# Down projection's operands on the weight plan, steps between units, last units by banks, attention's factor at the output

## The chip, the cores and the metric

The kernel runs on one core of a Trainium2 chip. A core has a matrix engine (PE in the profile; PEld is its weight load), a vector engine (DVE), a scalar engine (ACT), GpSimd (POOL) and a sync engine (SP). Here SP starts nearly all loads and stores, POOL starts those that add into their destination, and all of them are moved by the same 16 DMA engines. Matrix products are accumulated in PSUM, from where only DVE and ACT read them here. The metric is device time in microseconds; smaller is better.

## The reference, cut to what matters

One encoder layer on 512 tokens of width 2048, in float32:

```python
xn = rms_norm(x, attn_norm_g)
u_val, u_gate, q, k, v = split(xn @ w_in)              # 2048 x 5120
y_conv = silu(layer_norm(depthwise31(u_val * sigmoid(u_gate))))      # 1024 wide: group A
y_na = attention(q, k, v, rpb)   # 16 heads of 64, window 8 x 16 on an 8 x 64 grid: group B
x = x + concat(rms_norm(y_conv, conv_out_g), rms_norm(y_na, na_out_g)) @ w_out
gate, val = split(depthwise3(rms_norm(x, ffn_norm_g) @ w_up))         # 2048 x 11264
x = x + (silu(gate) * val) @ w_down                    # 5632 x 2048
return rms_norm(x, final_norm_g)
```

`rms_norm` divides every token's row by one number, so the factor of a token may as well be applied behind the matrix product that follows.

## The kernel before

Activations lie transposed (channels on partitions, 512 tokens along the free axis) up to the down projection, whose results lie with tokens on partitions. For accuracy every operand of a large product is split into a rounded high part and a rest, and a product is three matmuls (`mm3`, lines 126 to 128; `feed`, 728 to 730).

**Weights.** The weights come in units of 128 x 1024. `plan` is a list of functions, one for each unit in the order of use; `weights()` (147) hands out the next unit and first makes those up to `AHEAD = 3` further: a load by SP into one of seven `raw` buffers, the high part by ACT (L115) and the rest by DVE (L116), four buffers of each. A maker of the high part waits, where the buffer it writes is still read, for PE.

**Order.** The order of instructions on each engine comes from a scheduler that follows program order, priorities and its own estimates, so instructions that are written one behind the other may stand in another order, but each engine then works its list off strictly. Side work is written as generators in `steps` and `asteps`; `tick` (133) runs one step of each behind the last matmul of a unit.

**Stages.** (1) The input projection, 80 units in `project`; between them the convolution (`gated`, L311), group A's norms (`group_a`) and attention by head pairs (`attend`): `scores` takes both halves of a pair's scores into the two-bank PSUM tile `sc`, loads two bias tables `tab` by SP (L403), adds them (L407) and exponentiates; `turn` transposes, `values` multiplies by V. `attend` leaves its result in `aos`. (2) The output projection, `out_half(ma, read_a)` and then `out_half(mb, after)`, 16 units each. Between them `norm_b` computes the factor of group B's norm, multiplies the eight tiles of `aos` by it (L501) and splits them (L182, L183) into `mb`, the operands of the second half. `after` adds a product to `x2` (L540), squares it, transposes it to DRAM (`xt`) and makes the operands of (3). (3) The up projection, 44 blocks `f`, each as seven products of half size (a Strassen scheme) of 24 matmuls; then the convolution of width 3, silu and the product with the gate. The first 36 results go to DRAM by SP (L667), the last eight stay; `again` brings the 36 back during the last block by SP (L678). (4) The down projection, again seven products, each of 22 units; `product2` takes a unit and its `operand` (L708 on ACT, L709 on DVE, with one to three sums ahead of them), multiplies it into four PSUM banks, and takes the last `TAIL = 3` units bank by bank. Between products the results are added to the residual (`onto`, L754), and for finished ones `ready` squares (L773) and scales by the norm's weights (L774), `write` computes the token factors (L778 to L785), scales (L791 on DVE, L793 on ACT) and stores by SP (L795). All of this is written between the calls of `product2`.

The sums of two quarters of `w_down` that the scheme needs are made in DRAM by POOL: `sum_ahead` (170) issues a copy and an accumulating load (L176, L177), 88 jobs in all, one behind each of two in three units of the input projection, each second unit of the output projection and each block of the up projection until none is left.

Of the kernel before, what the change touches and what calls it, by code (L numbers as in the profile page):

```python
# [10 lines left out]
F32 = mybir.dt.float32  # L11
F32R = mybir.dt.float32r
AF = mybir.ActivationFunctionType
# [3 lines left out]
P = 128  # L17
# [35 lines left out]
Q = D // 2 // S  # L53
TAIL = 3
ROW = 2048
# [15 lines left out]
def layer(ctx: ExitStack, tc: tile.TileContext, xT, w_in, w_out, w_up, w_down, par, tab, g3, out):  # L71
# [17 lines left out]
    def t2(name, dt=F32):  # L89
        return tp.tile([P, S], dt, tag="t2k", name=name)  # L90
# [181 lines left out]
    def project(n):  # L272
        ps = psm.tile([P, S], F32, tag="mm", name="pj")
        for u in range(KD // U):
            w = weights()
            for k in range(U):
                kk = u * U + k
                m = mm3(ps, w, k, xs[kk][0], xs[kk][1], kk == 0, kk == KD - 1)
            tick(m)
            if weights.at > 6 and weights.at % 3:  # L280
                sum_ahead(m)
            while late:
                late.pop()()
        return ps
# [63 lines left out]

    aos = []
    acc_na = t2("accna")  # L350
# [26 lines left out]
    def attend(p, q, k, v):  # L377
# [14 lines left out]
        def scores(b0):  # L392
# [8 lines left out]
            for j in range(2):  # L401
                tb = t2("tab").rearrange("p (i k) -> p i k", i=2)
                i = nc.sync.dma_start(tb, tab[2 * p + j][:, b0 // 2:b0 // 2 + 2])  # L403
                if p == 0:
                    pin(i)
                s = t2("s").rearrange("p (i k) -> p i k", i=2)
# [27 lines left out]
        def values(b0):  # L434
            for i in range(2):
                b = b0 + i
                for ch in range(2):
                    for j in (1, 0):
# [3 lines left out]
                        if (i, ch, j) != (0, 0, 1):  # L442
                            pin(m)

        yield
        scores(0)
        yield
        yield
        scores(2)
# [46 lines left out]
    mb, wait = [], []  # L496
# [103 lines left out]
    for c in TURN2:  # L600
        for k in order2:
            plan.append(lambda c=c, k=k: unit(wsum[c][k] if c in wsum else w_down[k, {0: A22, 3: A11, 5: A12}[c]],
                                              U * P))

# [65 lines left out]

    back = [f for p in range(2) for f in range(p, NF - KEEP, 2)]

    def again(at, i):
        for _ in range(8):
            if back:
                f = back.pop(0)
                hs[f] = t2("h")
                behind(nc.sync.dma_start(hs[f], hd[f]), i)  # L678

    def paced(at, i):  # L680
        if at == 3:
            sum_ahead(i)

    for f in range(NF):
        hidden(f, again if f == NF - 1 else paced)
    assert not jobs and not back

    def operand(c, k):  # L690
# [19 lines left out]
        return t  # L710

    def four(first):

        if first:
            b = psa.tile([P, 2, S], F32, tag="sc", name="pd2")
            return [psa.tile([P, S], F32, tag="tr", name="pd", bufs=2) for _ in range(2)] + [b[:, 0], b[:, 1]]
        return [psm.tile([P, S], F32, tag="mm", name="pd") for _ in range(3)] + [psa.tile([P, S], F32, tag="po",
                                                                                         name="pd")]

    def product2(c, ps, more):  # L720
        got = []

        def feed(w, h, i, start, stop):
# [5 lines left out]
            nc.tensor.matmul(ps[i], h[:, t], wl[:, d], start=False, stop=False, skip_group_check=more)  # L729
            nc.tensor.matmul(ps[i], h[:, tl], wh[:, d], start=False, stop=stop, skip_group_check=more)  # L730
# [20 lines left out]

    def onto(x, ps):
        for a, b in zip(x, ps):
            add(a, a, b)  # L754
        return x

    gs = []
    for d in range(2 * Q):
        g = t2("g3")
        nc.sync.dma_start(g, g3[:, d * S:(d + 1) * S])  # L760
        if d >= Q:
            nc.vector.tensor_scalar(g, g, -1.0, None, op0=ALU.mult)
        gs.append(g)

    sq = [sm.tile([P, 2, 2 * Q], F32, tag="sq", name="sq") for _ in range(2)]

    def ready(y, th, dh):

        for i in range(2 * Q):
# [6 lines left out]
    def write(th, ys):  # L776
        v, r, y = (sm.tile([P, 2], F32, tag="rs" + c, name="rs" + c) for c in "vry")
        nc.vector.tensor_reduce(v, sq[th], axis=AX.X, op=ALU.add)  # L778
        nc.vector.tensor_scalar(v, v, 1.0 / D, EPS, op0=ALU.mult, op1=ALU.add)
# [5 lines left out]
        nc.vector.tensor_mul(y, y, r)  # L785
        for i in range(2 * Q):
            t, d = divmod(i, Q)
            for dh in range(2):
                x, f = ys[dh][i], y[:, t:t + 1]
                if dh:  # L790
                    nc.vector.tensor_scalar(x, x, f, None, op0=ALU.mult)  # L791
                else:
                    nc.scalar.activation(x, x, AF.Copy, scale=f)  # L793
                o = (Q * dh + d) * S
                nc.sync.dma_start(out[(2 * th + t) * P:(2 * th + t + 1) * P, o:o + S], x)  # L795

    a = four(True)
    product2(3, a, False)
    e3 = onto(rest(0, 0), a)
    b = four(False)  # L800
    product2(0, b, False)
    e0 = onto(rest(0, 1), b)
    product2(4, a, True)
    e4 = onto(rest(1, 0), a)
    b = four(False)
    product2(1, b, False)
    e1 = onto(rest(1, 1), b)
# [72 lines left out]
```

## Time and profile before

| | |
|---|---|
| median of 3 runs | 2069.67 us (2060.13 to 2070.61) |
| profiled execution | 2068.41 us |
| its span, first to last instruction | 2066.6 us |
| PE busy | 2011.7 us (97%) |
| DVE busy | 1588.8 us (77%) |
| ACT busy | 1019.7 us (49%) |
| moved by DMA | 445 MB, mean 215 GB/s |

"Busy" of PE is no measure of speed: a matmul's record overlaps the next, and its length doubles where the granted clock is halved. So the stages are read by windows: so many matmuls in so many microseconds, at such a clock. A wait row names the waiting instruction, then what ended the wait, the total, the count and the longest.

### The profile page before, as it was taken

How to read it: one execution, taken by the hardware profiler on the slowest of the kernel's cores; microseconds unless marked ns; L12 is line 12 of the kernel's file. 1: busy time of each engine (PE TensorE's matmuls, PEld its weight loads, DVE VectorE, ACT ScalarE, POOL GpSimd, SP SyncE). 2: the span in 40 equal slices, each digit the busy share in tenths (PEclk: the TensorE clock that was granted, in tenths of full speed). 3: DMA queues.
4: the chain of work that ended last, by engine and by line, in shares of the span. 5: the costliest groups of instructions: out<-in, count | busy, mean ns of one | idle time of the engine just before them, and what ended most of it. 6: DMA issues, size and time to landing. Idle time of an engine off the chain costs nothing.

```text
span 2066.6 us, 32277 instructions
## 1 busy us (share of the span) xinstructions
PE 2011.7 (97%) x12620; PEld 1799.9 (87%) x12620; DVE 1588.8 (77%) x2201; ACT 1019.7 (49%) x1548; POOL 202.8 (10%) x270
## 2 busy tenths in 40 slices
PE   8999999999999999999999999999999899999897
PEld 6878888877777899999999999999999688888776
DVE  7985797586566778888888888888888798874764
ACT  6234424446435655555545555554545544554553
POOL 0111111111111111111111100000010000000000
PEclk9999999999999999999999999999999999999999
DMA  6688788778868989998999977677677965666462
GB/s 230 183 242 215 195 214 210 216 198 250 246 165 217 237 229 244 255 242 247 250 253 243 247 189 201 190 193 202 182 188 205 334 208 200 207 211 203 160 214 95
DMA packets 143689, 444.97 MB, mean 215 GB/s; under 512 B 15792, under 2 KB 23984, under 8 KB 142128
## 3 DMA queue, kind: packets, MB, share of 16 engines
q1 hardware_dynamic: 104112, 304.48, 43.0%
q0 software_dynamic: 39424, 138.43, 32.6%
q8 instruction: 99, 1.62, 0.3%
q14 instruction: 54, 0.44, 0.1%
HBM read 425.02 MB, written 110.10 MB: 259 GB/s over the span
## 4 chain that ended last, share of the span: by engine, by line
PE 91%; DVE 4%; DMA 2%; ACT 1%; issue 1%; SPq 0%; ACTq 0%; DVEq 0%
PE pu L126 14%; PE pu L127 14%; PE pu L128 14%; PE pd L728 7%; PE pd L729 7%; PE pd L730 7%; PE pj L126 6%; PE pj L128 5%; PE pj L127 5%; PE po L126 3%; PE po L127 3%; PE po L128 3%; DMA tab<-in_tab 2%; DVE y L311 1%; DVE wlo L116 1%
## 5 line engine op out<-in xcount | busy, mean ns | idle before, releaser
L115 ACT ACTIVATE whi<-raw 128x1024 fp32r<-128x1024 f32 x574 | 605.1, 1057 | 824.9 <-PE pj L127 216.3
L116 DVE TENSOR_TENSOR wlo<-raw,whi 128x1024 fp32r<-128x1024 f32 x574 | 700.6, 1223 | 283.0 <-ACT whi L115 247.6
L126 PE MATMUL pu<-xc,whi 128*128 128x256 f32 x2464 | 697.3, 283 | 1.3 <-ACT uu L633 1.3
L127 PE MATMUL pu<-xc,whi 128*128 128x256 f32 x2464 | 697.7, 283 | 0.0
L128 PE MATMUL pu<-xc,wlo 128*128 128x256 f32 x2464 | 697.2, 283 | 0.0
L126 PEld LDWEIGHTS pu<-xc,whi 128*128 128x128 f32 x2464 | 473.0, 192 | 1.7 <-ACT uu L633 1.7
L127 PEld LDWEIGHTS pu<-xc,whi 128*128 128x128 f32 x2464 | 473.0, 192 | 0.4 <-issue 0.2
L128 PEld LDWEIGHTS pu<-xc,wlo 128*128 128x128 f32 x2464 | 473.0, 192 | 0.2 <-issue 0.2
L728 PE MATMUL pd<-whi,ho 128*128 128x512 f32 x616 | 242.6, 394 | 19.6 <-ACT ho L708 19.6
L126 PE MATMUL pj<-xh,whi 128*128 128x512 f32 x640 | 253.5, 397 | 8.2 <-ACT whi L115 8.2
L128 PE MATMUL pj<-xh,wlo 128*128 128x512 f32 x640 | 250.0, 391 | 1.1 <-DVE wlo L116 1.0
L127 PE MATMUL pj<-xl,whi 128*128 128x512 f32 x640 | 250.7, 392 | 0.0
L729 PE MATMUL pd<-wlo,ho 128*128 128x512 f32 x616 | 242.0, 393 | 0.0
L730 PE MATMUL pd<-whi,ho 128*128 128x512 f32 x616 | 241.2, 393 | 0.0
L311 DVE SCALAR_TENSOR_TENSOR y<-ch,prm,y 128x507 f32<-128x507 f32 (+14 forms) x240 | 169.8, 739 | 3.1
L728 PEld LDWEIGHTS pd<-whi,ho 128*128 128x128 f32 x616 | 117.2, 190 | 44.9 <-ACT ho L708 20.7
L126 PEld LDWEIGHTS pj<-xh,whi 128*128 128x128 f32 x640 | 120.5, 188 | 36.5 <-ACT whi L115 9.5
L128 PEld LDWEIGHTS pj<-xh,wlo 128*128 128x128 f32 x640 | 120.5, 188 | 28.3 <-DVE wlo L116 2.5
L127 PEld LDWEIGHTS pj<-xl,whi 128*128 128x128 f32 x640 | 120.6, 188 | 24.4 <-issue 0.7
L730 PEld LDWEIGHTS pd<-whi,ho 128*128 128x128 f32 x616 | 116.7, 190 | 25.3 <-DVE ho L709 1.1
L729 PEld LDWEIGHTS pd<-wlo,ho 128*128 128x128 f32 x616 | 117.1, 190 | 24.3
L177 POOL DMA_DIRECT2D ws<-in_w_down x88 | 79.1, 899 | 483.2 <-DMA ws<-in_w_down 270.8
(158 smaller groups left out, 2017.6 us busy)
## 6 DMA issues: line engine op xcount, KB each, us to landing
raw<-in_w_up SPq DMA_DIRECT2D x220, 512.0 KB, 5.1
ws<-in_w_down POOLq DMA_DIRECT2D x132, 512.0 KB, 7.0
raw<-in_w_up POOLq DMA_DIRECT2D x88, 512.0 KB, 7.6
raw<-ws SPq DMA_DIRECT2D x88, 512.0 KB, 4.3
raw<-in_w_in SPq DMA_DIRECT2D x80, 512.0 KB, 5.4
raw<-in_w_down SPq DMA_DIRECT2D x66, 512.0 KB, 4.3
ws<-ws POOLq DMA_DIRECT2D x44, 512.0 KB, 6.0
raw<-in_w_out SPq DMA_DIRECT2D x32, 512.0 KB, 5.2
```

The lines of the kernel that those rows point to most:

```text
L115: i = nc.scalar.activation(hi[:, :n], raw[:, :n], AF.Copy)
L116: j = nc.vector.tensor_sub(lo[:, :n], raw[:, :n], hi[:, :n].bitcast(F32))
L126: nc.tensor.matmul(ps, hi[:, a], mh, start=start, stop=False, skip_group_check=more)
L127: nc.tensor.matmul(ps, hi[:, a], ml, start=False, stop=False, skip_group_check=more)
L128: return nc.tensor.matmul(ps, lo[:, a], mh, start=False, stop=stop, skip_group_check=more)
L177: nc.gpsimd.dma_start(wsum[c][k], w_down[k, b], accum_op=ALU.add, max_dma_last_dim=ROW)
L311: nc.vector.scalar_tensor_tensor(y[:, a:b], h[:, a + j - PAD:b + j - PAD], prm[:, o + j:o + j + 1], y[:, a:b], op0=ALU.mult, op1=ALU.add)
L728: nc.tensor.matmul(ps[i], h[:, t], wh[:, d], start=start and not more, stop=False, skip_group_check=more)
L729: nc.tensor.matmul(ps[i], h[:, t], wl[:, d], start=False, stop=False, skip_group_check=more)
L730: nc.tensor.matmul(ps[i], h[:, tl], wh[:, d], start=False, stop=stop, skip_group_check=more)
```

## The change

- `operand(c, k)` moves into `plan`: it is made with its weight unit, three units before use, from within the last block of the up projection on.
- What follows a product of the down projection (`taken`, `ready`, `write`, and the loading of the norm's weights, `factors3`) is written as generators and run a step behind each unit of the next product.
- Only the last product is ended bank by bank, over `TAIL = 4` units; a bank's result is finished and, after each second bank, 128 tokens are normalised and stored while the other banks are multiplied. `write` handles 128 tokens, not 256. `four(True)` lists the two-bank tile first. Half of the stores go by POOL (`queues`), and the 36 loads of `again` too.
- `norm_b` only computes the factor; each `attend` splits its result at once, and `after` multiplies each product by the factor (new L547) before adding.
- The bias tables are loaded one step before the scores that they are added to (`table`).
- `sum_ahead` is called behind each second unit of the input projection and each third of the output projection, so more of its jobs fall into the up projection.

```diff
-            if weights.at > 6 and weights.at % 3:
+            if weights.at > 6 and weights.at % 2:
                 sum_ahead(m)
...
-                tb = t2("tab").rearrange("p (i k) -> p i k", i=2)
-                i = nc.sync.dma_start(tb, tab[2 * p + j][:, b0 // 2:b0 // 2 + 2])
+                tb = tabs.pop(0)
...
+        table(0)
         yield
         scores(0)
         yield
+        table(2)
         yield
         scores(2)
...
-        aos.append(ao)
+        mb.append(split(ao, pc("nag", p), "mb"))
...
-            if d % 2:
+            if d % 3 == 0:
                 sum_ahead(i)
...
-        r = yield from rsqrt_steps(acc_na, NA, "rna")
-        for i in range(NP_):
-            nc.vector.tensor_mul(aos[i], aos[i], r)
-            mb.append(split(aos[i], pc("nag", i), "mb"))
+        rb.append((yield from rsqrt_steps(acc_na, NA, "rna")))
...
-        nc.vector.tensor_add(x2[d], x2[d], ps)
+        t = t2("oa")
+        nc.vector.tensor_mul(t, ps, rb[0])
+        nc.vector.tensor_add(x2[d], x2[d], t)
...
-            plan.append(lambda c=c, k=k: unit(wsum[c][k] if c in wsum else ..., U * P))
+            plan.append(lambda c=c, k=k: (unit(wsum[c][k] if c in wsum else ..., U * P), operand(c, k)))
...
-                behind(nc.sync.dma_start(hs[f], hd[f]), i)
+                behind(nc.gpsimd.dma_start(hs[f], hd[f]), i)
...
-            return [psa.tile(...) for _ in range(2)] + [b[:, 0], b[:, 1]]
+            return [b[:, 0], b[:, 1]] + [psa.tile(...) for _ in range(2)]
...
-        n = NK - TAIL
-        for j, k in enumerate(order2[:n]):
-            w, h = weights(), operand(c, k)
+        n = NK - TAIL if c == TURN2[-1] else NK
+        for j in range(n):
+            w, h = weights()
             for i in range(2 * Q):
-                feed(w, h, i, j == 0, False)
-        got = [(weights(), operand(c, k)) for k in order2[n:]]
-        for i in range(2 * Q):
-            for j, (w, h) in enumerate(got):
-                feed(w, h, i, False, j == TAIL - 1)
+                m = feed(w, h, i, j == 0, j == NK - 1)
+            tick(m)
+        if n < NK:
+            got = [weights() for _ in range(NK - n)]
+            for i in range(2 * Q):
+                for j, (w, h) in enumerate(got):
+                    feed(w, h, i, False, j == NK - n - 1)
+                yield i
...
+    def ready(x, ps, th, dh, only=range(2 * Q)):
+        for i in only:
             t, d = divmod(i, Q)
             d += Q * dh
+            add(x[i], x[i], ps[i])
             q = t2("sq")
-            nc.scalar.activation(q, y[i], AF.Square, accum_out=sq[th][:, t, d:d + 1])
-            nc.vector.tensor_mul(y[i], y[i], gs[d])
+            nc.scalar.activation(q, x[i], AF.Square, accum_out=sq[th][:, t, d:d + 1])
+            nc.vector.tensor_mul(x[i], x[i], gs[d])
+            yield
+
+    queues = [nc.sync, nc.gpsimd]
...
-                nc.sync.dma_start(out[(2 * th + t) * P:(2 * th + t + 1) * P, o:o + S], x)
+                queues[dh].dma_start(out[(2 * th + t) * P:(2 * th + t + 1) * P, o:o + S], x)
+                yield
...
-    product2(2, a, True)
-    for y, th in ((e0, 0), (e1, 1)):
-        ready(onto(y, a), th, 1)
-    product2(6, b, True)
-    ready(onto(e4, b), 1, 0)
+    run(2, a, True)
+    steps += [ready(e0, a, 0, 1), ready(e1, a, 1, 1)]
+    run(6, b, True)
+    steps += [ready(e4, b, 1, 0), write(1, 0, (e4, e1)), write(1, 1, (e4, e1))]
     a = four(True)
-    write(1, (e4, e1))
-    product2(5, a, False)
-    ready(onto(e3, a), 0, 0)
-    write(0, (e3, e0))
+    for i in product2(5, a, False):
+        for _ in ready(e3, a, 0, 0, (i,)):
+            pass
+        if i % Q == Q - 1:
+            for _ in write(0, i // Q, (e3, e0)):
+                pass
```

More of the change, by code (lines that the diff above doesn't have):

```diff
@@ L53 @@
 Q = D // 2 // S
-TAIL = 3
+TAIL = 4
 ROW = 2048
@@ L443, in values, with table @@
                             pin(m)
+        tabs = []
+        def table(b0):
+            for j in range(2):
+                tb = t2("tab").rearrange("p (i k) -> p i k", i=2)
+                i = nc.sync.dma_start(tb, tab[2 * p + j][:, b0 // 2:b0 // 2 + 2])
+                if p == 0:
+                    pin(i)
+                tabs.append(tb)
+        table(0)
         yield
@@ L601, in layer @@
         for k in order2:
[L602 to L603 removed]
+            plan.append(lambda c=c, k=k: (unit(wsum[c][k] if c in wsum else w_down[k, {0: A22, 3: A11, 5: A12}[c]],
+                                               U * P), operand(c, k)))
     out_half(mb, after)
@@ L669, in hidden @@
             hs[f] = g
[L671 to L677, printed above, removed]
-                behind(nc.sync.dma_start(hs[f], hd[f]), i)
[L680 to L686, printed above, removed]
     def operand(c, k):
@@ L710, in operand, with again, paced @@
         return t
+    back = [f for p in range(2) for f in range(p, NF - KEEP, 2)]
+    def again(at, i):
+        for _ in range(8):
+            if back:
+                f = back.pop(0)
+                hs[f] = t2("h")
+                behind(nc.gpsimd.dma_start(hs[f], hd[f]), i)
+    def paced(at, i):
+        if at == 3:
+            sum_ahead(i)
+    for f in range(NF):
+        hidden(f, again if f == NF - 1 else paced)
+    assert not jobs and not back
     def four(first):
@@ L715, in four @@
             b = psa.tile([P, 2, S], F32, tag="sc", name="pd2")
-            return [psa.tile([P, S], F32, tag="tr", name="pd", bufs=2) for _ in range(2)] + [b[:, 0], b[:, 1]]
+            return [b[:, 0], b[:, 1]] + [psa.tile([P, S], F32, tag="tr", name="pd", bufs=2) for _ in range(2)]
         return [psm.tile([P, S], F32, tag="mm", name="pd") for _ in range(3)] + [psa.tile([P, S], F32, tag="po",
@@ L785, in write, with run, then @@
         nc.vector.tensor_mul(y, y, r)
[L786 to L787 removed]
+        for d in range(Q):
             for dh in range(2):
[L789 removed]
+                x = ys[dh][t * Q + d]
                 if dh:
[L791 removed]
+                    nc.vector.tensor_scalar(x, x, y, None, op0=ALU.mult)
                 else:
[L793 removed]
+                    nc.scalar.activation(x, x, AF.Copy, scale=y)
                 o = (Q * dh + d) * S
[L795 removed]
+                queues[dh].dma_start(out[(2 * th + t) * P:(2 * th + t + 1) * P, o:o + S], x)
+                yield
+    def run(c, ps, more):
+        for _ in product2(c, ps, more):
+            pass
+    def then(*g):
+        for x in g:
+            yield from x
     a = four(True)
[L798 to L799 removed]
+    steps.append(factors3())
+    run(3, a, False)
+    e3 = rest(0, 0)
+    steps.append(taken(e3, a))
     b = four(False)
[L801 to L804, printed above, removed]
[L805 to L817 removed]
+    run(0, b, False)
+    e0 = rest(0, 1)
+    steps.append(taken(e0, b))
+    run(4, a, True)
+    e4 = rest(1, 0)
+    steps.append(taken(e4, a))
+    b = four(False)
+    run(1, b, False)
+    e1 = rest(1, 1)
+    steps.append(taken(e1, b))
+    run(2, a, True)
+    steps += [ready(e0, a, 0, 1), ready(e1, a, 1, 1)]
+    run(6, b, True)
+    steps += [ready(e4, b, 1, 0), write(1, 0, (e4, e1)), write(1, 1, (e4, e1))]
+    a = four(True)
+    for i in product2(5, a, False):
[3 more added lines that the diff above has]
+            for _ in write(0, i // Q, (e3, e0)):
+                pass
 def _cols(a):
```

39 lines of the change are left out of this document (18 added, 21 removed).

## The prediction

> **What bounds the kernel now.** I read the page's first part, then windows by stage, then PE's waits, then the timeline at each wait.
>
> ```profile
> span 2066.6 us, 32277 instructions
> PE 2011.7 (97%) x12620; PEld 1799.9 (87%) x12620; DVE 1588.8 (77%) x2201; ACT 1019.7 (49%) x1548; POOL 202.8 (10%) x270
> ```
>
> Windows: length, then each engine's busy time and count, granted PE clock, DMA share and rate.
>
> ```profile
> core 0: us, PE busy (x) PEld busy (x) DVE busy (x) ACT busy (x) POOL busy (x), PEclk, DMA share, GB/s
> 732.00:1170.00 438.00, 438.00 (x3647) 437.54 (x3646) 361.12 (x412) 228.07 (x306) 69.60 (x87) 1.00 0.93 247
> 1170.00:1608.00 438.00, 438.00 (x3653) 438.00 (x3651) 361.27 (x409) 226.44 (x303) 34.78 (x40) 1.00 0.73 199
> 1617.00:1622.70 5.70, 5.68 (x13) 4.44 (x14) 1.73 (x5) 5.02 (x17) 0.00 (x0) 0.50 1.04 399
> 1630.00:1918.00 288.00, 288.00 (x1272) 238.50 (x1271) 227.86 (x377) 139.00 (x196) 0.00 (x0) 1.00 0.62 210
> ```
>
> The up projection runs at 438/3647 = 0.120 us for each 256-wide matmul from end to end, the down projection at 288/1272 = 0.2264 us for a 512-wide one; behind a long wait the clock is 0.50 and a matmul takes 5.70/13 = 0.44 us. PE is the bound, and only what is not at this pace can be won:
>
> ```profile
> 142.90:144.10 1.20, 0.51 (x4) 0.10 (x4) 1.20 (x3) 1.20 (x4) 0.00 (x0) 1.00 1.27 437
> 451.40:454.40 3.00, 0.98 (x5) 0.35 (x4) 1.38 (x3) 1.71 (x6) 0.00 (x0) 1.00 0.83 307
> 503.40:514.00 10.60, 6.49 (x26) 4.59 (x24) 4.92 (x9) 4.84 (x13) 0.88 (x1) 0.68 0.98 316
> 531.90:534.50 2.60, 1.15 (x9) 0.48 (x9) 1.23 (x1) 2.32 (x4) 0.47 (x1) 1.00 0.76 291
> 598.80:606.00 7.20, 3.67 (x10) 2.60 (x10) 6.93 (x11) 1.67 (x2) 0.41 (x1) 0.76 0.84 216
> 1607.90:1623.00 15.10, 6.32 (x17) 4.84 (x17) 8.50 (x15) 8.86 (x22) 0.00 (x0) 0.66 1.04 390
> 1918.90:1931.00 12.10, 5.14 (x15) 3.48 (x14) 11.82 (x21) 10.97 (x32) 0.00 (x0) 0.72 0.37 119
> 1987.90:1996.00 8.10, 4.20 (x14) 2.91 (x13) 7.79 (x16) 7.55 (x18) 0.00 (x0) 0.79 0.62 174
> 2053.70:2066.60 12.90, 0.02 (x1) 0.00 (x0) 5.32 (x15) 4.10 (x9) 0.00 (x0) 0.61 0.43 163
> ```
>
> Where the clock stayed at 1.00 the loss is the idle time: 0.7, 2.0 and 1.4 us. Elsewhere it is the length less the work at full pace (the first two of a count began before the window): at 598.8, 7.2 - 8 x 0.2264 = 5.4; at 1607.9, 15.1 - 14 x 0.2264 - 0.12 = 11.8; at 1918.9, 12.1 - 13 x 0.2264 = 9.2; at 1987.9, 8.1 - 12 x 0.2264 = 5.4; at 503.4, with eight 512-wide and sixteen small matmuls at 0.12, 10.6 - 3.7 = 6.9. The last 12.9 us have no matmul. PE's waits name the causes:
>
> ```profile
> PE pd L728 <- ACT ho L708: 19.6, 3, 8.8
> PE sc L397 <- DVE s L407: 4.1, 1, 4.1
> PE po L126 <- DVE oa L509: 3.5, 1, 3.5
> PE st L326 <- DVE su L413: 2.0, 1, 2.0
> ```
>
> **The change part by part. First unit of the down projection (11.8 us).** ACT, then DVE:
>
> ```profile
> 1608.16 1.06 ACT L115 ACTIVATE whi<-raw 128x1024 fp32r<-128x1024 f32 x1 [1.77 <-PE pu L127]
> 1616.57 1.32 ACT L708 ACTIVATE ho<-uy 128x256 fp32r<-128x256 f32 x4
> 1609.25 1.22 DVE L116 TENSOR_TENSOR wlo<-raw,whi 128x1024 fp32r<-128x1024 f32 x1 [1.60 <-ACT whi L115]
> 1617.31 1.43 DVE L709 TENSOR_TENSOR ho<-uy,ho 128x256 fp32r<-128x256 f32 x4
> ```
>
> The operand stood behind the whole tail of the last block, though the first product reads only even-numbered results, here kept ones that were long there. In the built order of the changed program the first three operands stand right behind the fourth unit's `whi` on ACT and `wlo` on DVE, not ahead of them. That `whi` still waits for the end of the last up unit (1608.16 to 1609.2). So the first operand's high part is there at about 1609.6, its rest at 1609.25 + 1.22 + 0.4 = 1610.9: PE stands about 1.5 us, then 0.8 before the third matmul, and 2.3 of the 11.8 stay. Idle stretches of 1.4 and 2.0 us left the clock at 1.00 above, so no slow matmuls. The block's tail (1610.4 to 1617.3) now runs beside three units of 12 x 0.2264 = 2.7 us; the fourth operand would be some tenths early. Gain 9.5; if PE has to wait for that one too, 7; if nothing waits, 11.8.
>
> **What follows a product (9.2 and 5.4).** Operands 110 to 113 and 132 to 135 now stand ahead of the squares and adds on ACT and DVE, which are spread behind units. No work is added; DVE is busy 227.86 of 288 us in this stage. The add of the first bank (0.7) comes ahead of the rest of the unit that is needed 8 us later. Both go: 14.6. If an add or square stands at the wrong place, one unit's 2.7 us is lost at each of six borders, a bound of 16 that I leave to a rival.
>
> **The end (12.9).**
>
> ```profile
> 2053.76 1.29 DVE L754 TENSOR_TENSOR xr<-xr,pd 128x512 f32<-128x512 f32 x2 [1.87 <-PE pd L730]
> 2058.07 2.56 ACT L793 ACTIVATE xr<-xr,rsy 128x512 f32<-128x512 f32 x4 [1.02 <-DVE rsy L785]
> 2058.59 4.47 SPq L795 DMA_DIRECT2D out_T<-xr  x8
> out_T<-xr SPq DMA_DIRECT2D x16, 256.0 KB, 3.0
> L176 POOL DMA_DIRECT2D ws<-ws x44 | 26.4, 601 | 224.4 <-PE pu L128 91.9 <-DMA ws<-in_w_down 72.1 <-PE po L128 31.1
> ws<-ws POOLq DMA_DIRECT2D x44, 512.0 KB, 6.0
> ```
>
> The factors came 4.4 us after the last matmul, then four scalings on an engine (2.56) and eight stores by SP (4.47). In the new order the last bank's add stands on DVE behind the first half's chain, which ends about then, and the half's last small steps and scalings (2 us) stand ahead of the last reduction: the factor of the second half comes at about +4.9 us, no earlier. But only two scalings an engine are left and two stores a queue: the last POOL store is issued at about +6, lands some 3.5 later (taken: nearest 3.0 of SP with the same size; 6.0 is the row of POOL with double the size in a busy stage), and 1.2 us pass to the end of the span as now. That is +10.6, a gain of 2.3; with 6.0 us, -0.2; with 3.0, 2.8. The Trainium skill (DMA: Bandwidth & Descriptors, section SWDGE vs HWDGE vs iDMA) speaks against this part: it puts plain copies on SP or ACT, since descriptors for GpSimd's are made by a program that DVE's fast mode can lock out. No run here shows that lock; by that rule the second rival below holds.
>
> **Bias tables (0.7, 2.0 and 6.9).** DVE's wait for them, their landing, and two steps of the chain of waits:
>
> ```profile
>   DMA tab<-in_tab: 21.2, 11
> DMA to landing us min/median/max: 4.2/6.2/13.3
> 445.28 7.71 DMA tab<-in_tab
> 493.81 13.30 DMA tab<-in_tab
> ```
>
> Loaded a unit (5.4 us) earlier, they cover a median landing. The 0.7 goes. The statistics matmul at 451 needs the score tile that the second table held up; it stands eight matmuls earlier now, so about 0.4 stays: 1.6. At 503 SP still issues the tables only behind a weight load that waits for a buffer which group A frees, and DMA is full there; but both stand together, where two 512 KB loads stood between them. I take 2.5 of 6.9 to stay: gain 4.4, ends 0 and 6.9. The wait at 532, where ACT copies behind a `whi`, keeps its order: 1.4 stays.
>
> **Factor at the output (5.4).**
>
> ```profile
> 598.85 1.32 DVE mbl L183 x2
> L509 DVE TENSOR_TENSOR oa<-po,ra 128x512 f32<-128x512 f32 x16 | 10.9, 684 | 10.3 <-PE po L128 10.0 <-ACT ra L219 0.2
> 626.00:717.00 91.00, 91.00 (x424) 72.59 (x423) 64.69 (x123) 57.36 (x109) 14.43 (x19) 1.00 0.88 227
> ```
>
> The eight multiplications and splits held up DVE before the second half; they are gone or spread, so 5.4 goes. In return 16 multiplications of 0.684 us enter the second half: DVE goes from 64.7 to 75.6 of 91 us, beside PE. The last pair's chain into the up projection is 0.7 longer, of which PE feels about 0.5. Ends 0 and 10.9.
>
> **Sums and loads on POOL.** The calls in the input projection fall from 50 to 37, in the output projection from 16 to 12, so they last until block 39 instead of 22. The two windows of the up projection show the price: with them 247 GB/s and 0.1201 us a matmul, without them 199 GB/s and 0.1199. Nothing. The 36 loads of `again` cost POOL at most 0.9 us each, 32 us from 1591 on; from unit 5 on an even one is needed each 2.7 us, the odd ones a product later. Nothing.
>
> **Sum.** 0.7 + 1.6 + 4.4 + 5.4 - 0.5 + 9.5 + 14.6 + 2.3 = 38.0 us. The profiled execution took 2068.41 (span 2066.6 and 1.8 around it): 2030.4, so 2030. The median of the runs, 2069.67, is 1.3 above that execution; against it the gain is 1.9%.
>
> **The rivals.** (1) The tables come no earlier at 451 and 503, since SP works its list strictly: both terms fall away, 2030 + 6 = 2036. The 13.30 speaks for it, the shorter queue against. (2) POOL's stores at the end land as its rows in busy stages do, 6 us, and the end gains nothing: 2033. (3) DVE becomes the bound in the second half of the output projection: at 83% of the time a chain of waits can fall behind PE: 2030 + 10.9 = 2041. (4) The change does not do what it says: ACT's operands stand behind a `whi` that waits for PE at each border, as at the first unit, and the three starts keep their 26.4 less 2.3: 2054. (5) Slower: with sums in blocks 22 to 38 too, the accumulating loads of POOL come late behind them and PE waits. It decides from (38 + 10.3)/17 = 2.8 us a block; the first window, with the same load and not a single wait, speaks against it: 2080.
>
> **How the numbers follow.** Chances: forecast 0.50, (1) 0.15, (2) 0.12, (3) 0.08, (4) 0.06, (4) with (3), 2065, 0.05, (5) 0.04. About 0.5% (10.3 us) is what a measurement of this kernel can tell from no change. Faster 0.91, same 0.05, slower 0.04. The range runs from all residues gone (2.3 + 0.4 + 2.5 + 0.5, and 1 or 2 more at the end: 2021 or 2022) to (3) and a little beyond, 2044.
>
> **What would show it.** Right: no PE wait for `ho` above 2 us; clock 1.00 at the borders of products; no wait for DVE before the second half; about 10.5 us behind the last matmul; the up projection at 0.120 throughout. Wrong: PE waits for ACT or DVE at unit 3 or at the borders, a table landing later than the scores, matmuls slower than 0.2264 or waits of `po` in the second half, PE waits in blocks 22 to 38, or a POOL store landing last and late.

## The result and the profile after

The changed kernel takes 2036.93 us (median of 4 runs, 2035.26 to 2037.69) against 2070.14 us in the same comparison: a ratio of 0.9849, 95% interval 0.9818 to 0.9880. The gain is 33.2 us; 38 were forecast, and the forecast time was 2030.4. The profiled execution took 2037.69 us with a span of 2035.9, which is 30.7 us shorter than the span of before.

First the head of its page, then PE's waits (what waited, what ended the wait, total, count, longest):

```profile
span 2035.9 us, 32324 instructions
PE 2005.8 (99%) x12620; PEld 1795.3 (88%) x12620; DVE 1593.5 (78%) x2223; ACT 1017.6 (50%) x1548; POOL 227.7 (11%) x314
```

```profile
PE sc L397 <- DVE s L404: 3.1, 1, 3.1
PE pd L737 <- DVE ho L698: 2.2, 2, 1.6
PE trv L385 <- ACT pt L428: 1.4, 1, 1.4
PE pd L735 <- ACT ho L697: 1.3, 1, 1.3
```

The 19.6 us of waits for `ho`, the operands of the down projection, are down to 3.5. The windows at the places that lost time before:

```profile
core 0: us, PE busy (x) PEld busy (x) DVE busy (x) ACT busy (x) POOL busy (x), PEclk, DMA share, GB/s
142.00:143.20 1.20, 1.20 (x10) 0.77 (x10) 1.13 (x3) 1.06 (x4) 0.00 (x0) 1.00 0.51 195
448.40:451.40 3.00, 2.55 (x10) 1.49 (x9) 2.91 (x7) 1.83 (x8) 0.00 (x0) 1.00 1.05 197
498.50:509.00 10.50, 7.43 (x37) 5.58 (x36) 7.20 (x12) 6.74 (x20) 0.91 (x1) 0.84 1.00 339
581.00:595.00 14.00, 14.00 (x62) 11.21 (x61) 6.41 (x9) 3.44 (x4) 1.07 (x2) 1.00 0.53 135
1599.20:1607.00 7.80, 5.91 (x19) 4.27 (x19) 4.69 (x9) 2.62 (x5) 2.70 (x6) 0.78 1.02 398
1619.90:1626.00 6.10, 4.50 (x19) 3.10 (x18) 3.71 (x8) 2.12 (x2) 0.00 (x0) 1.00 0.96 359
1904.00:1908.00 4.00, 4.00 (x19) 3.31 (x18) 4.00 (x6) 2.97 (x8) 0.00 (x0) 1.00 0.56 186
1964.00:1968.00 4.00, 4.00 (x19) 3.34 (x18) 4.00 (x7) 3.04 (x8) 0.00 (x0) 1.00 0.44 164
2025.00:2035.90 10.90, 0.05 (x1) 0.00 (x0) 4.70 (x19) 3.52 (x7) 2.16 (x4) 0.69 0.52 192
```

PE is busy without a gap at the middle of the output projection (581) and at both borders of products (1904, 1964). Four places still lose time: 498, the first unit of the down projection (1599), a new one at 1620, and the wait of 1.4 us for ACT (`pt`, at 528 now), which the prediction left as it was.

Both kernels issue the same 12,620 matmuls, so the trace can be cut at the same matmul in each. A cut such as "pd 120" is the start of the 120th matmul into the down projection's tile. The table gives the time between cuts; all later comparisons use it, since the total hides a gain in one place behind a loss in another.

| stretch (from cut to cut) | before | after | change | forecast |
|---|---|---|---|---|
| start to pj 541 | 140.43 | 140.12 | -0.31 | 0 |
| pj 541 to 601 (the wait at 143) | 17.62 | 16.85 | -0.77 | -0.7 |
| pj 1701 to 1801 (451) | 32.17 | 31.12 | -1.05 | -1.6 |
| pj 1801 to po 260 (503) | 54.80 | 52.23 | -2.57 | -4.4 |
| po 560 to 669 (before the second half) | 30.43 | 24.70 | -5.73 | -5.4 |
| po 669 to 1020 (second half) | 88.18 | 90.00 | +1.82 | +0.5 |
| pu 200 to 7392 (up projection) | 863.04 | 863.04 | 0 | 0 |
| pu 7392 to pd 120 (first units of the down projection) | 39.02 | 33.33 | -5.69 | -9.5 |
| pd 1300 to 1360 (first border) | 22.79 | 13.60 | -9.19 | -9.2 |
| pd 1580 to 1640 (second border) | 19.09 | 13.60 | -5.49 | -5.4 |
| pd 1640 to the end of the span | 60.46 | 58.79 | -1.67 | -2.3 |

The rows left out change by 0.11 us or less. The first row is no gain: in the twelve profiles of the experiments the first matmul of the input projection starts anywhere from 7.5 to 8.9 us. And some 0.46 us of the -5.73 and of the +1.82 only moved from one row to the next: the first four transposes of `x2` stand just ahead of the cut at po 669 before, and just behind it after. Without them the two rows change by -5.3 and +1.4.

**The new wait at 1620.** DVE's timeline there (start, length, engine, line, operation; in brackets the idle time before and what ended it):

```profile
1612.51 1.22 DVE L116 TENSOR_TENSOR wlo<-raw,whi 128x1024 fp32r<-128x1024 f32 x1
1613.65 0.42 DVE L698 TENSOR_TENSOR ho<-h,ho 128x256 fp32r<-128x256 f32 x1
1613.98 1.22 DVE L116 TENSOR_TENSOR wlo<-raw,whi 128x1024 fp32r<-128x1024 f32 x1
1621.18 0.43 DVE L770 TENSOR_SCALAR g<-g 128x512 f32<-128x512 f32 x1 [5.98 <-DMA g<-in_g]
1621.52 0.42 DVE L698 TENSOR_TENSOR ho<-h,ho 128x256 fp32r<-128x256 f32 x1
```

`factors3` loads the norm's weights in the first product and changes the sign of two of the four tiles on DVE. That small instruction waited 5.98 us for its load, and the rest of unit 6's operand (L698), whose data was there, stood behind it. The weights aren't used before the fifth product has ended.

### The profile page after: what moved, and what is told of

Same layout as the page of the kernel before. It is cut to its first block, busy times and chain, and to the rows that moved or that the text cites. A ratio compares the mean times of both kernels' runs of the same rounds, so it can differ in the third digit from the quotient of the medians.

```text
span 2035.9 us, 32324 instructions
## 1 busy us (share of the span) xinstructions
PE 2005.8 (99%) x12620; PEld 1795.3 (88%) x12620; DVE 1593.5 (78%) x2223; ACT 1017.6 (50%) x1548; POOL 227.7 (11%) x314
## 4 chain that ended last, share of the span: by engine, by line
PE 76%; issue 21%; ACT 1%; DMA 1%; DVE 1%; POOL 0%; SPq 0%; POOLq 0%; DVEq 0%
PE pu L126 15%; PE pu L127 15%; PE pu L128 15%; PE pj L126 7%; PE pj L128 6%; PE pj L127 6%; PE po L126 3%; PE po L127 3%; PE po L128 3%; PE po L437 1%; PE sc L397 1%; PE trp L424 1%; DMA raw<-in_w_in 1%; DMA tab<-in_tab 0%; PE trx L537 0%
```

## The experiments

All are compared stretch by stretch with the changed kernel.

**u1: operands made at their use.** The spread steps stay.

```diff
-            plan.append(lambda c=c, k=k: (unit(...), operand(c, k)))
+            plan.append(lambda c=c, k=k: unit(...))
...
-            w, h = weights()
+            w, h = weights(), operand(c, order2[j])
```

> The changed kernel with one part undone: an operand of the down projection is again made where its unit is used, not three units ahead; the spread steps, the last units by banks and all else stay. Theory (the borders and the first unit were lost to operands that stood behind other work): the first unit waits again for the tail of the last block, about 11.8 us lost there against 5.9 in the changed kernel, so +6; at the borders before unit 110 and unit 132 the operands stand between the adds and squares, and a wait of 1 to 2 us comes back at each: +2 to +4. Together 8 to 10 us longer. Rival (spreading the steps alone won the borders, and the operands' place matters only at the first unit): no PE wait for an operand at either border, +6. Rival (the place of the operands does nothing): 0.

Measured 2042.87 us in one run (before, beside u1 to u4: 2064.21). The last matmul of the up projection to the first of the down projection takes 6.89 us instead of 1.61; the first border takes 13.64, the stretch behind it, pd 1360 to 1580, 50.27 instead of 49.87, and the second border 13.60. So 5.3 us at the first unit and 0.4 us around the borders: the first rival. The place of the operands alone doesn't make the borders.

**u2: what follows a product issued at once.** The operands stay three units ahead.

```diff
-    steps += [ready(e0, a, 0, 1), ready(e1, a, 1, 1)]
+    now(ready(e0, a, 0, 1), ready(e1, a, 1, 1))
```

and the same for the other calls (`now` runs its generators to their end).

> The changed kernel with one part undone: the adds, squares and multiplications that follow a product, the token factors and the loading of the norm's weights are issued at once between two products, not a step behind each unit. The operands stay three units ahead. Theory: behind product 2 eight adds and eight multiplications of 0.68 us and a wlo (12.5 us on DVE) stand ahead of operand 113, which is needed 8.5 us after the border: a wait of about 4 us, and some slow matmuls; behind product 6 half as much stands ahead of operand 135, 7.8 us, needed at 8.5: no wait. Some 4 to 6 us longer in all. Rival (operands three units ahead are enough): 0. Rival (without the spread the old losses of 9.2 and 5.4 are back): +14.

Measured 2043.59 us. PE loses 1.07 us up to pd 1360 and 0.66 right behind it, both at operand 113, and nothing at the second border: the place that I expected, but less than my 4 to 6. The sixteen adds and multiplications take DVE from 1908.73 to 1918.49 us, 0.61 us each and not the 0.68 of a single row, since the end of one overlaps the next. The larger loss lies where I hadn't looked: pd 1 to 120 takes 35.26 us instead of 31.72. Both sign changes stand in one piece there:

```profile
1616.58 0.43 DVE L770 TENSOR_SCALAR g<-g 128x512 f32<-128x512 f32 x1 [4.14 <-DMA g<-in_g]
1618.63 0.43 DVE L770 TENSOR_SCALAR g<-g 128x512 f32<-128x512 f32 x1 [1.63 <-DMA g<-in_g]
1618.98 0.75 DVE L698 TENSOR_TENSOR ho<-h,ho 128x256 fp32r<-128x256 f32 x2
```

PE waits 5.5 us for that operand.

**e5: both undone.**

> The changed kernel with the edits of u1 and u2 together: operands made at their use, and what follows a product issued at once. Either alone lost less than 2 us at the two borders. Theory (each of the two is enough by itself, since either lets the first operands of a product come ahead of the adds): with neither, operand 110 stands behind eight adds, eight multiplications and a wlo on DVE (16 x 0.68 + 1.22 = 12 us), and the borders lose about 10 and 5 us again, 15 together, with the first unit's 5 to 7 beside it. Rival (a product whose last units are not taken bank by bank has no such loss, so the third edit won the borders): under 4 us at the two borders.

Measured 2060.88 us in one run (before, beside e5 to e8: 2067.98). The borders take 25.37 and 18.90 us against 13.60 each: 11.8 and 5.3 us lost, 17.1 together; the first units (pu 7392 to pd 120) take 40.49 us, 7.2 more. DVE at the first border of this kernel, then PE's waits for `ho` in all of it:

```profile
1915.27 1.87 DVE L787 TENSOR_TENSOR xr<-xr,pd 128x512 f32<-128x512 f32 x3
1917.07 1.89 DVE L790 TENSOR_TENSOR xr<-xr,g 128x512 f32<-128x512 f32 x3
1918.87 0.68 DVE L787 TENSOR_TENSOR xr<-xr,pd 128x512 f32<-128x512 f32 x1
1919.47 1.22 DVE L116 TENSOR_TENSOR wlo<-raw,whi 128x1024 fp32r<-128x1024 f32 x1
1920.61 0.68 DVE L790 TENSOR_TENSOR xr<-xr,g 128x512 f32<-128x512 f32 x1
1921.21 1.42 DVE L698 TENSOR_TENSOR ho<-uy,ho 128x256 fp32r<-128x256 f32 x4
```

```profile
PE pd L735 <- ACT ho L697: 21.9, 3, 9.7
```

The first operand comes behind all sixteen adds and multiplications. So the two parts do the same thing at the borders: each alone saves 15.3 to 16.6 us there, and the other adds only the 0.4 or 1.7 us of u1 and u2. That a product's last units are no longer taken bank by bank is not what won it, since that stayed changed here.

**u3: the factor before the second half.**

```diff
-        rb.append((yield from rsqrt_steps(acc_na, NA, "rna")))
+        r = yield from rsqrt_steps(acc_na, NA, "rna")
+        for i in range(NP_):
+            nc.vector.tensor_mul(aos[i], aos[i], r)
+            mb.append(split(aos[i], pc("nag", i), "mb"))
```

> The changed kernel with one part undone: the factor of group B's norm is again multiplied into the eight tiles before the second half of the output projection, and the 16 multiplications behind its products are gone. Theory from the two traces: the wait before the second half is back (+5.2 us), and the second half, which is 1.7 us slower in the changed kernel than before, wins these back: 3.5 us longer. Rival (the 1.7 us have nothing to do with the 16 multiplications): +5.2 with the slow second half.

Measured 2036.35 us. po 669 to 1020 takes 88.26 us, as before. Of the 1.7 us more in the changed kernel 0.46 are the four transposes that moved across the cut. The other 1.3 come with the 16 multiplications, at the transposes of `x2`: a group of them starts 0.43 us behind the matmul ahead of it in the mean of 15 groups, 0.33 in u3 and 0.34 before. PE's weight loads for them idle 6.5 us in all, 5.1 in the kernel before (the waits of after, then of before, over this half):

```profile
PEld trx L537 <- issue: 5.8, 13, 0.5
PEld trx L537 <- DVE x L548: 0.7, 2, 0.3
```

```profile
PEld trx L531 <- ACT whi L115: 2.3, 7, 0.3
PEld trx L531 <- issue: 2.2, 6, 0.4
PEld trx L531 <- DVE x L540: 0.6, 2, 0.3
```

In the changed kernel most of it names no cause (`issue`); that it is the later sum for which PE waits is argued from u3, where the lag goes with the multiplications.

The wait in the middle is back, 3.5 us, but po 560 to 669 takes only 28.98 us against 30.43 before, since the clock stayed at 1.00 behind it, and the wait of 1.4 us for ACT at 527 is gone (po 260 to 560: 67.87 instead of 69.49). Over the whole output projection, po 260 to 1020, undoing this part costs 185.11 - 184.20 = 0.9 us, not the 3.5 I expected. Some 1.5 us of the difference is the luck of the clock (last section), and 1.6 the wait at 527, which the kernel before had too; why it goes here stays open.

**u4: tables loaded with their scores.**

```diff
-                tb = tabs.pop(0)
+                table(b0, j)
+                tb = tabs.pop(0)
```

> The changed kernel with one part undone: each bias table is again loaded with the scores that use it. Theory (all that was won at 143, 451 and 503 us is the earlier load): 0.6 + 1.6 + 2.2 = 4.4 us longer, and the waits for the score tile are back at their old length. Rival (fewer sums of POOL in the input projection, 37 instead of 50, made the tables land sooner): 0 to 2 us longer.

Measured 2035.82 us: no loss. The wait at 143 is back (17.39, +0.54), pj 1701 to 1801 is shorter (30.57, -0.55), and pj 1801 to po 260 takes 51.47 us, among the 50.0 to 53.9 us of the kernels with the early load. The theory falls. The size fits the rival, whose cause e4 and e6 test.

**e4: the sums at the old pace.**

```diff
-            if weights.at > 6 and weights.at % 2:
+            if weights.at > 6 and weights.at % 3:
...
-            if d % 3 == 0:
+            if d % 2:
```

> The changed kernel with one edit: the sums on POOL at the old pace (50 in the input projection, 16 in the output projection, done by block 22). Theory (they cost nothing where they are): 0, within 1 us, and the up projection as long as in the changed kernel. Rival (the lighter load helps the tables land): 1 to 3 us longer around 500 us. Rival (sums in blocks 22 to 38 cost the up projection): shorter there, by 0.5 us or more.

Measured 2039.80 us. pj 1801 to po 260 takes 55.59 us, longer than in any kernel with the new pace and like the 54.80 of before; pu 200 to 7392 takes 863.04 us again, and all else agrees. In the up projection the sums cost nothing; around 503 us they cost some 3 us. PE's wait before a score product there is 4.1 us (before) and 4.6 (e4) at the old pace and 1.8 to 3.4 in the eleven profiles with the new one. The rest of the difference is slow matmuls: the clock was halved for 6.83 us in both kernels with the old pace, for 0 to 3.41 with the new one, save e2 with 6.83. The stretch at 451 takes 31.14 us as in the changed kernel, 1.03 less than before, and the one at 143 takes 16.86, 0.76 less: there the earlier load wins its time at the old pace too.

**e6: the kernel before with the new pace alone.**

> The kernel before with one part of the change alone: sums behind each second unit of the input projection and each third of the output projection. Theory (formed from u4 and e4: the tables land sooner because POOL's sums take less of the DMA, not because they are asked for a unit earlier): the losses around 451 and 503 us fall by 1.6 and about 3 us, the one at 143 stays, and the up projection keeps its length: 4 to 5 us shorter than before. Rival (the earlier load of the tables is what counts): 0 to 1 us shorter.

Measured 2064.80 us in one run, within the 2063.69 to 2074.31 us of the kernel before; the stretches tell more. pj 1701 to 1801 takes 30.00 us (-2.17), pj 1801 to po 260 51.98 us (-2.82): 5.0 us by a change of two numbers. The span is only 3.6 us shorter, mainly because at the second border the clock was halved for 6.83 us and not 3.41, which cost 1.6 far behind the edit. At 143 us the pace wins 0.27. The wait of DVE for the tables, in the kernel before, in this one, and in e4, which asks early at the old pace:

```profile
DVE s L407 <- DMA tab<-in_tab: 21.2, 11, 4.2
```

```profile
DVE s L407 <- DMA tab<-in_tab: 11.1, 5, 5.0
```

```profile
DVE s L404 <- DMA tab<-in_tab: 9.2, 2, 5.1
```

Asking early takes away many short waits, and PE wins by it at 143 and 451 us (0.76 and 1.03 in e4). What is left in e4 is two long ones at 503, 5.1 us the longest, for tables that land late. So at 143 it is the earlier load that counts, at 451 either change alone wins what the two win together or more, and at 503 it is the pace. Windows 485 to 515 us of before and of e6:

```profile
485.00:515.00 30.00, 25.89 (x113) 20.21 (x112) 17.78 (x25) 17.35 (x34) 3.70 (x5) 0.89 0.92 289
```

```profile
485.00:515.00 30.00, 27.58 (x140) 22.31 (x139) 19.16 (x29) 20.22 (x42) 2.85 (x4) 0.94 0.83 272
```

The DMA share falls from 0.92 to 0.83.

**e1: sign changes in the second product.**

```diff
-            if d >= Q:
-                nc.vector.tensor_scalar(g, g, -1.0, None, op0=ALU.mult)
...
-    steps.append(taken(e3, a))
+    steps += [taken(e3, a), signs()]
```

> The changed kernel with one edit: the two sign changes of the final norm's weights, which on DVE wait for the load of these weights in the first product of the down projection, are moved to the second product. Theory: the 2.1 us that PE lost around unit 6 (a wait of 1.76 for the rest of an operand that stood behind this wait on DVE, and matmuls at half clock behind it) are gone, all else stays: 2.1 us shorter. Rival (the operands' data, loaded by POOL at 390 GB/s, come late too): the wait stays in part, less than 1 us won.

Measured 2032.85 us in one run (before, beside e1 to e4: 2065.12). The wait around unit 6 is gone, PE runs through:

```profile
1606.00:1619.00 13.00, 13.00 (x59) 10.79 (x58) 12.86 (x24) 11.65 (x26) 6.34 (x12) 1.00 1.03 390
1619.00:1626.00 7.00, 7.00 (x33) 5.79 (x32) 6.85 (x15) 2.67 (x4) 0.00 (x0) 1.00 1.03 399
```

The loads are as dense as in the changed kernel, and the operands' data was in time: the theory. pd 1 to 120 takes 27.94 us; it is 30.1 to 30.3 in e3, e4, u3 and u4, which have the wait and run at full clock, so 2.2 us.

**e2: e1, with the first four operands four units earlier** and the high parts of units 4 to 6 held behind the last block's convolution (`tail`).

```diff
+    for j in range(4):
+        plan[j - 4] = with_operand(plan[j - 4], order2[j])
...
+        if late:
+            with tc.issue_after(tail[-1].ins):
+                return parts(raw, n)[:2]
```

> The edit of e1, and the first four operands of the down projection made four units earlier, ahead of the weights that wait for the end of the up projection; the weights of units 4 to 6 stand behind the tail of the last block. Theory: the two waits of 1.5 and 0.7 us at the first unit and the half clock behind them (1.7 us) are gone, so 3.9 us less than e1, 6 us less than the changed kernel. Rival (the tail of the last block then runs late, and operand 4 or the weights of unit 4 come after their unit): a wait of 1 to 3 us at unit 4 or 5, with 1 to 3 us won. For the clock: if the half clock comes from the short waits, it is gone with them; if it comes from the change of work, it stays.

Measured 2032.92 us, as long as e1, but only because pj 1801 to po 260 took 53.86 us here and 51.28 there, far ahead of the edit. The start of the down projection takes 0.12 us instead of 1.61, pd 1 to 120 27.00 instead of 27.94, and PE doesn't wait for `ho` at all: 2.4 us less than e1. No wait came back at units 4 or 5. The other 1.5 us that I expected were slow matmuls, of which e1 had none.

**e3: all stores by SP.**

```diff
-    queues = [nc.sync, nc.gpsimd]
+    queues = [nc.sync, nc.sync]
```

> The changed kernel with one edit: all 16 stores of the output by SP, none by POOL. Theory (the price is how many stores a queue issues behind the last factor): SP issues four in the last half instead of two, at about 0.5 us each: the end is 0.6 to 1.0 us longer, 11.5 to 11.8 instead of 10.85. Rival (stores by POOL are slow, as the Trainium skill has it for plain copies): the end is shorter than 10.85.

Measured 2035.20 us. From the last matmul's start to the end 11.01 us instead of 11.26: shorter, against my theory. SP issues its stores some 0.46 us apart, so the last goes out later, 6.5 us behind the last matmul instead of 5.9, but they land in 2.5 us. The nine other profiles with both queues take 11.26 to 11.29 us there, e7, with SP alone, 11.03. The stores of the end in the changed kernel and in e3:

```profile
out_T<-xr SPq DMA_DIRECT2D x4, 256.0 KB, 2.9
out_T<-xr POOLq DMA_DIRECT2D x4, 256.0 KB, 3.4
```

```profile
out_T<-xr SPq DMA_DIRECT2D x8, 256.0 KB, 2.5
```

With two queues SP's own stores land later too, 2.9 against 2.5, so POOL and the crowd are not told apart. No run of the changed kernel ends the last product as the kernel before does, so what its end by banks is worth is read from the trace alone.

**e7: the best of these, and e8, the changed kernel beside it.** e7 has e2, e3, and no sums around 500 us:

```diff
-            if weights.at > 6 and weights.at % 2:
+            if 75 > weights.at > 6 and weights.at % 2:
...
-            if d % 3 == 0:
+            if d % 3 == 0 and weights.at > 82:
```

> The changed kernel with the edits of e2 (sign changes late, four operands first) and e3 (stores by SP), and no sums at all between unit 75 of the input projection and the second unit of the output projection (45 sums ahead of the up projection, 43 in it). Theory: 2.2 + 2.4 + 0.25 us by the first three, and 1 to 2 of the 2.3 to 3.5 us that are left around 500 us by the last: 6 to 7 us less than the changed kernel, about 0.3%. Rival (DMA is full around 500 us with the loads of weights alone): the last gives nothing, 5 us.

> The changed kernel as it is, on the chip of e7, to compare with. The wait of 1.5 and 0.7 us at the first unit of the down projection is there again; behind it the matmuls are at full pace if the half clock in the first profile of this kernel was chance (seven of eight other runs with the same wait had none), else at half.

Measured over three rounds with 2067.98 us before: e8 2035.86 us (ratio 0.9840, interval 0.9818 to 0.9863), e7 2027.33 us (0.9797, 0.9779 to 0.9816). e7 is 8.5 us shorter than e8. Of this, pj 1801 to po 260 gives 1.4 us (48.57 against 50.02, the shortest of all kernels), the first units of the down projection 6.1 (27.12 against 33.25 from pu 7392 to pd 120), of which 1.5 are slow matmuls that e8 had, and the end 0.2; 0.6 more lie in the start, which differs between executions. Without the slow matmuls e7 is 7.0 us shorter, at the upper end of the 6 to 7 expected. That the sums left out around 500 us give the 1.4 is likely and not shown: one profile, where kernels with the same pace spread over 50.0 to 53.9 us. In e8 the clock fell at the first unit again (the other profiles with that wait and a full clock were six, not seven); the last section shows what decides it:

```profile
1599.20:1606.00 6.80, 6.25 (x21) 4.70 (x20) 4.68 (x10) 1.97 (x4) 2.58 (x6) 0.75 1.03 400
```

## Why the prediction was right, and where it was wrong

The forecast was a gain of 1.9%, the measured one is 1.5%; the time lay inside the range, 6.5 us above the forecast. The low end of that range does not follow from its own terms: 2030 less 5.7 and less 1 or 2 is 2022 or 2023, not 2021 or 2022. Point by point:

- **Borders: right in size, incomplete in cause.** 14.6 forecast, 14.7 measured. The step said that the operands now stand ahead and that the adds are spread; e5 with u1 and u2 shows that either would have done.
- **The wait before the second half: right** (5.4 forecast, 5.3 measured without the moved transposes). The step "16 multiplications of 0.684 us enter the second half", "beside PE", with about 0.5 us felt by PE, was too low: 1.4 measured, of which u3 gives 1.3 to the multiplications. I looked at DVE's total and at the last pair, and not at the transposes behind each product. The third rival, DVE as the bound with 10.9 us, came, if at all, as this small part. And the wait that went is not what the whole part is worth: undoing it cost u3 only 0.9 us.
- **The end: right in time, a little short in gain** (2.3 forecast, 1.7 measured). Forecast 10.6 us behind the last matmul, the last POOL store issued at about +6 and landing 3.5 later; measured 10.9, with that store issued at 2030.94 (+5.9) and landing at 2034.67 (3.7). Behind the last matmul's start 2.05 us were won (13.31 to 11.26); the last product took 0.4 longer ahead of it, mostly at three late matmuls of its end by banks. The second rival, 6 us to land, did not come. The Trainium skill (DMA: Bandwidth & Descriptors, section SWDGE vs HWDGE vs iDMA), which puts plain copies on SP or ACT, agrees with e3 in direction: 0.25 us.
- **First unit: mis-sized, 9.5 forecast and 5.7 measured.** The two waits came as forecast, 1.5 and 0.73 us. Two things were missing. The change adds the sign changes of `factors3` to the first product, a wait for a DMA on DVE ahead of an operand; the part-by-part account costed the spread steps as "no work is added" and never listed this one: 2.2 us by e1. And "Idle stretches of 1.4 and 2.0 us left the clock at 1.00 above, so no slow matmuls" failed in the profiled execution: ten matmuls at half clock, 1.6 us. The length of a wait is not what decides this (last section); whether the 1.6 us come is chance from one execution to the next.
- **Tables: the cause was wrong where most was forecast.** "Loaded a unit (5.4 us) earlier, they cover a median landing", 6.7 us in all, of which 4.4 came. At 143 us this holds (0.77). At 451 the earlier load wins 1.03 at the old pace (e4), but the new pace alone wins more (2.17 in e6, 1.60 in u4), and with both it is 1.05 again. At 503, where 4.4 was forecast and 2.57 came, e4 and e6 show that the pace of the sums did it, a part that the prediction put at "Nothing" from two windows of the up projection. In that stage it is nothing (863.04 us with either pace). The sums that were taken away stood in another stage, where DMA is full (a share of 0.92 around 500 us) and a table is late, and there I did not ask. Beside the new pace the earlier load is worth nothing in sum (u4). The first rival, that the tables come no earlier, is half right: DVE waits for them at 503 as before (3.55 and 1.41 us, 2.84 and 3.01 before), but no longer at 451 (2.59 before).
- **Up projection: right**; the fifth rival (sums in blocks 22 to 38) did not show, nor did the fourth at the borders.

In sum: 38.0 - 3.8 (first unit) - 2.3 (tables) - 0.9 (second half) - 0.6 (end) - 0.1 (the factor's wait) + 0.5 (the start 0.3, small stretches 0.2) = 30.8, against the 30.7 between the spans. What stays open: how much of the 503 stretch is the sums alone, since with the same pace it took 50.0 to 53.9 us from one execution to the next, and up to 6.83 us of half clock stand in it.

## What to carry to other kernels

Before a step is moved into side work, list each of its instructions that waits for a DMA and see what stands behind it on the same engine: a sign change of 0.43 us cost 2.2 us here, because operands stood behind it. When two parts of a change serve the same wait, undo each alone and both together; u1 and u2 by themselves would have told that neither matters at the borders. And to price traffic that is taken away, look at the stage from which it is taken, not at the one to which it goes.

## What the runs showed of the hardware

**What decides whether a wait halves PE's clock.** The same wait left the clock alone in one execution and halved it in another. The pair of 1.5 and 0.73 us at the first unit stands in eight of these profiles (the changed kernel twice, u2, u3, u4, e1, e3, e4); in six the matmuls behind it ran at 1.00, in two, both of the changed kernel as it is, at half clock for some 3.4 us. The 3.5 us wait before the second half has both outcomes too: in u3 it left the clock alone,

```profile
591.80:599.00 7.20, 3.66 (x16) 2.71 (x16) 6.92 (x11) 1.67 (x2) 1.40 (x2) 1.00 0.61 220
```

while before, the same 7.2 us had a granted clock of 0.76 and 10 matmuls, not 16. The Trainium skill (TensorE: Matmul & The Clock Gate, Part 1: The HAM clock gate) says that the clock falls after an idle window of about 3.4 us that runs free of the program, so that the outcome of a wait depends on where it meets the window. The traces agree on the window. In each of the 14 profiles all changes of the granted clock, from the first one at 11 to 15 us on, lie whole multiples of 3.413 us apart, to 0.02 us (in the kernel before, twelve changes up to 2057 us), and where this grid lies differs from one execution to the next. They do not agree that the window has to be idle; here the measurement decides. Rows cut by the grid: the pair in the changed kernel, in e8 and in e1, then the 3.5 us wait in the kernel before and in u3:

```profile
1599.02:1602.43 3.41, 1.52 (x8) 0.88 (x7) 1.87 (x4) 1.98 (x4) 0.87 (x2) 1.00 1.02 396
1602.43:1605.84 3.41, 3.41 (x9) 2.62 (x9) 2.82 (x7) 0.00 (x0) 1.60 (x3) 0.50 1.02 395
```

```profile
1596.60:1600.01 3.41, 1.67 (x10) 1.03 (x9) 1.81 (x3) 1.98 (x4) 0.93 (x2) 1.00 1.02 394
```

```profile
1596.99:1600.40 3.41, 2.07 (x14) 1.51 (x13) 1.81 (x2) 1.98 (x4) 0.89 (x3) 1.00 1.01 390
1600.40:1603.82 3.42, 2.87 (x13) 2.34 (x13) 3.42 (x9) 0.19 (x1) 1.50 (x3) 1.00 1.03 399
```

```profile
599.09:602.50 3.41, 0.16 (x1) 0.00 (x0) 3.41 (x5) 1.64 (x2) 0.12 (x1) 1.00 0.70 151
```

```profile
590.66:594.08 3.42, 1.57 (x7) 0.95 (x6) 3.42 (x5) 1.67 (x2) 0.51 (x1) 1.00 0.27 96
594.08:597.49 3.41, 1.72 (x8) 1.45 (x9) 3.41 (x7) 0.00 (x0) 0.00 (x0) 1.00 0.98 352
```

PE's busy share of the window tells the cases apart. In the changed kernel and in e8 the whole pair, in e8 all but its last 0.15 us, falls into one window, with PE busy for 45% and 49% of it, and the next window runs at half clock. In the six others a border of the grid parts the pair, or more work shares its window, and no window is below 60%. The 3.5 us wait left 5% of one window in the kernel before, and 46% and 50% of two in u3. Over all profiles, from 16 us on, 8231 windows ran at full clock: behind each of the 24 with PE busy for 45% or less the clock was halved, behind none above 50%, and behind two of the four between. So what these traces show is that half a window of work, about 1.7 us in 3.41, keeps the clock; the length of a single wait does not decide, and which of the eight executions paid 1.6 us was a matter of where the grid lay. The shares rest on the profile's ends of matmuls, which are modelled.
